# Moving two depthwise-convolution tiles from GpSimd to TensorE, tying row transposes to expert products, and adding repeated products in two norm pauses

## The chip, the cores and the metric

The kernel runs on one core of one Trainium2 chip. The metric is the device time of one execution in microseconds (us). The engines are called as in the profile: PE (TensorE), DVE (VectorE), ACT (ScalarE), POOL (GpSimd) and SP (SyncE, which here only issues transfers).

## The reference, cut to what matters

All tensors are float32. Two blocks run one after the other on 512 tokens of width 1024; the first one puts 16 meta tokens in front, so that it works on 528 rows.

The first block has two layers. Each projects the rows onto ten parts, and computes beside an indexer, a top-132 selection and an eight-head attention over the selected keys a convolution branch:

```python
def conformer_conv_branch(a, g, z, w_dw, b_dw, ln_g, ln_b):
    u = a * jax.nn.sigmoid(g)                      # 512 channels
    u = lax.conv_general_dilated(u, w_dw[:, None, :], window_strides=(1,),
        padding=[(30, 0)], feature_group_count=512, ...) + b_dw   # 31 taps
    u = jax.nn.silu(layer_norm(u, ln_g, ln_b))
    return u * jax.nn.silu(z)
...
    y = concatenate([y_conv, y_attn]) @ w_out[l]
    h = layer_norm(DEEPNORM_ALPHA * h + y, post_ln_g[l], post_ln_b[l])
```

The second block is one layer of windowed attention and a gated linear attention, then 16 experts, each of which takes the 64 tokens with the highest affinity to it (gate, up and down matrices of 1024 x 1024 each, 201 MB in all), and a gated per-token embedding.

## The kernel before

The 512 convolution channels of a layer are four tiles of 128 channels (partitions) by 528 or 512 positions. The phase `p_ag(c)` projects a and g of tile c (two projections of 48 fp32r products each) and forms `u`. From there a tile goes one of two ways. If c stands in `pconv`, `conv_tap` makes 31 taps: ACT scales a shifted view of `u` by the tap (line 333), and POOL adds the result onto `cv` (line 335); two `prod` buffers lie between them, so that ACT waits at the third tap that POOL has not taken. Otherwise `conv_operands(c)` makes 16 tiny products (line 346), one DVE product of 128 x 1024 (line 348), writes `u` to DRAM and reads it back in eight pieces with the positions shifted (lines 354 to 360, all issued by SP), and later `conv_products(c)` runs 64 fp32 products in four column groups of PE (lines 261 and 267, through `burst`) and one ACT copy (line 376). The operands of such a tile lie in buffers that exist once (`szc`, `k2l`, `side`); `szc` is also where the gate of the branch (`p_zc`) is put.

A planner in the compiler orders the instructions of each engine ahead of the run, by simulated times and by levels: of the instructions that are ready it takes the one of the highest level, and within a level the one that was written first. Each engine then runs its list strictly in order. `self.plan` gives each layer the order of its levels, the order of its phases, and `pconv`. In layer 0 the levels are `w, topk, tail, idx, proj, conv, att, ag, rest, fill`; in layer 1 `w, tail, idx, conv, proj, att, ag, topk, rest, fill`. `p_ag(c)` stands in level `ag` (after attention) if c is in `pconv`, and in `proj` (before it) if not. After the phases comes the tail: a one-element `warm` activation on `cv` of the last `ag` tile of the phase order (`clast`), a Sqrt that makes ACT load its square-root table ahead of need, the layer norm of the branch, the output projection, and the post norm.

In the experts, pair j of two experts needs its 128 token rows gathered by POOL (`gather_rows`, line 1500) and turned on PE (`gather_cols`, line 1507). These tasks are written at fixed steps of the loop over weight pieces: the turns for pair j four steps ahead of its gate products. The rows of pair 0 come from a product with a one-hot matrix instead (`first_rows`, line 1495). The expert products are line 1643; two products of 64 columns run side by side. Expert weights stream through SP into every buffer that has come free.

Of the kernel before, what the change touches and what calls it, by code (L numbers as in the profile page):

```python
# [23 lines left out]
KT = D // 128  # L24
# [45 lines left out]
class Net:  # L70
    def __init__(self, tc, I, out, dbg=None, upto=99):
        self.tc, self.nc, self.I, self.out, self.dbg = tc, tc.nc, I, out, dbg
        self.upto = upto
        self.bgq = []
        self.plan = [
            (('w', 'topk', 'tail', 'idx', 'proj', 'conv', 'att', 'ag', 'rest', 'fill'),
             ('ag0', 'idx', 'q', 'k', 'sc', 'ag3', 'v', 'cp3', 'ag2', 'ag1', 'topk', 'zc', 'att', 'za'),
             (2, 0, 1, 3),
             (2, 3, 1, 0),
             (0, 1, 2)),  # L80
            (('w', 'tail', 'idx', 'conv', 'proj', 'att', 'ag', 'topk', 'rest', 'fill'),
             ('idx', 'q', 'k', 'sc', 'ag2', 'v', 'cp2', 'ag3', 'ag1', 'cp3', 'ag0', 'topk', 'att', 'za', 'zc'),
             (2, 0, 1, 3),
             (2, 3, 1, 0),
             (0, 1)),
        ]
        self.order2 = ('w', 'crit', 'att', 'gla', 'main', 'late', 'fill')
        self.gn0, self.apull, self.gpull, self.ng = 2, 3, (1, 0, 2, 1), 0
        self.early = ("qk", "qk", "u", "szc", "cv", "qi", "xl", "xl", "parts", "v", "c1", "sm", "sm", "one", "raw", "raw", "raw", "hw", "hl")
        self.last = ("raw", "u", "szc", "qi")  # L90
        self.cycle = ("qk", "qk", "u", "szc", "cv", "qi", "xl", "xl", "v", "sm", "sm", "one", "raw", "raw", "raw", "hw", "hl")
        self.piece = 264
        self.swap = True
        self.stack = True
        self.sqsum, self.sqe, self.xlp = 'v', 'AAAAAAAA', ()
        self.pairs2 = False
        self.pairs, self.spare = False, None
        self.cur = None
        self.pos = 0
# [181 lines left out]
    def layer(self, l):  # L281
        nc, I = self.nc, self.I
# [3 lines left out]
        T = L - q0  # L286
# [218 lines left out]
        v = self.sb([128, 4, 512], "v")  # L505
# [199 lines left out]
                tmp = self.sb([128, T], "th", "rl", 3)  # L705
                self.silu2(seg(szc[0][:, e, :]), ps, seg(tmp))

        phases = dict(cp2=lambda: conv_products(2), cp3=lambda: conv_products(3), ag0=lambda: p_ag(0), ag1=lambda: p_ag(1), ag2=lambda: p_ag(2), ag3=lambda: p_ag(3), idx=p_idx, sc=p_scores, topk=p_topk, k=p_k, q=p_q, v=p_v, att=p_att, za=p_za, zc=p_zc)
        for n in seq:
            phases[n]()  # L710

# [12 lines left out]
        for t in range(nt):  # L724
            ps = self.ps([128, 512], "tp")
            for c in range(4):
                nc.tensor.transpose(ps[:tw, c * 128:(c + 1) * 128], cv[:, c, t * tw:(t + 1) * tw], self.ident)
            x = self.sb([128, 512], "xct", "pT" if t < 4 else "rl", 4 if t < 4 else 3)
# [37 lines left out]
        for e, ps in self.proj_tiles(w_out, 0, D, y, KT, fsegs if q0 == 0 else ((0, S),), half=True):  # L766
            ot = self.sb([128, T], "ot", "rl", 3)
            for k in range(2):
                nc.vector.scalar_tensor_tensor(seg(ot), seg(hT[k][:, e, q0:].bitcast(F32)), ALPHA, ps if k == 0 else seg(ot),
                                               op0=ALU.mult, op1=ALU.add)  # L770
            ec = slice(e * 128, (e + 1) * 128)
            pt = self.ps([128, 4, 128], "tp")
            for i in range(4):
                c0 = NM - q0 + 128 * i
                nc.tensor.transpose(pt[:, i, :], ot[:, c0:c0 + 128], self.ident)
            nc.scalar.copy(z[:, :, ec], pt)
            for i in range(4):
                nc.vector.bn_stats(st[:, i, e, :], z[:, i, ec])
            if l == 0:
                pm = self.ps([NM, 128], "pm")  # L780
                nc.tensor.transpose(pm, ot[:, 0:NM], self.ident)
                nc.scalar.copy(zM[:, ec], pm)
                nc.vector.bn_stats(stM[:, e, :], zM[:, ec])
        mv = self.sb([128, 5, 2], "mv")
        sc = self.sb([128, 5, 2], "sc")
        nc.vector.memset(mv, 1.0)
# [566 lines left out]
    def experts(self, mx):  # L1353
        nc, I = self.nc, self.I
# [147 lines left out]
        def gather_cols(j, st):  # L1502
            xf = self.sb([128, KT, 128], "xf", "ya", 2)
            for g in range(2):
                pt = self.ps([128, 4, 128], "tp")
                for k in range(4):
                    nc.tensor.transpose(pt[:, k, :], st["xr"][:, g * 512 + k * 128:g * 512 + (k + 1) * 128], self.ident)
                gained(xf, pt, g, gf)
            xfs[j] = xf

# [106 lines left out]
        for kind, j in streams:  # L1617
            if (kind, j) == ("d", NP - 1):
                load_gate()
            rows_of = dict(p=128) if j == 0 and kind != "d" else dict(t=KT)  # L1620
            wv = [I[names[kind]][0, 2 * j + q].rearrange("(t p) f -> p t f" if "p" in rows_of else "(p t) f -> p t f", **rows_of) for q in range(2)]
            ps = None
            for t in range(0, KT, 2):
                run_tasks(step + 1)
                if (kind, j, t) == ("d", NP - 1, KT - 2):

                    two = [self.sb([128, 2, D], "rawe", "raw", 3) for q in range(2)]
                    raw = [[[two[q][:, k, :]] for k in range(2)] for q in range(2)]
                    for k in range(2):
                        for q in range(2):  # L1630
                            nc.sync.dma_start(raw[q][k][0], wv[q][:, t + k, :])
                else:
                    raw = [chunk(w, t) for w in wv]
                if ps is None:
                    ps = self.ps([128, 2, 512], "pp", "pp", 2)
                for k in range(2):
                    x = hids[j][(t + k) // 4][:, (t + k) % 4] if kind == "d" else xfs[j][:, t + k]
                    for s in range(2):
                        for q in range(2):
                            r = raw[q][k]  # L1640
                            r = r[s] if len(r) > 1 else r[0][:, s * 512:(s + 1) * 512]
                            a = slice(64 * q, 64 * q + 64)
                            nc.tensor.matmul(ps[a, s, :], x[:, a], r, start=(t == 0 and k == 0), stop=(t == KT - 2 and k == 1), skip_group_check=True)  # L1643
                step += 2
            if kind == "g":
                at_step(step, post_gate, j, ps)
            elif kind == "u":
                at_step(step + 2, post_up, j, ps)
            else:
                at_step(step, post_down, j, ps)  # L1650
                at_step(step, scat_init, j)
                for i in range(4 if j < NP - 1 else 0):
                    for s in range(2):
                        at_step(step + 2 + 2 * (i // 2), scat, j, i, s)
# [139 lines left out]
```

## Time and profile before

| | us |
|---|---|
| median of 3 runs (1835.46 to 1839.21) | 1838.72 |
| the profiled execution, its own time | 1837.06 |
| span of that execution, first to last instruction | 1835.2 |
| PE busy | 1688.8 |
| DVE busy | 931.9 |
| ACT busy | 766.7 |
| POOL busy | 219.8 |

A busy PE is not a PE at its peak, since the ends of pipelined products are modelled. Roughly: layer 0 runs to 383 us, layer 1 to 741, the second block's mixing to 1270, the experts from 1298 to 1770, and the gated embedding to the end. The mean granted PE clock was 0.97 of 2.4 GHz.

### The profile page before, as it was taken

The page shows a single profiled execution, that of the slowest core. Times are in us where ns is not written, and L with a number is a line of the kernel's source. Part 1 is how long each engine was busy: PE and PEld are TensorE (multiplying, and loading weights), DVE is VectorE, ACT ScalarE, POOL GpSimd, SP SyncE. Part 2 cuts the span into 40 slices and gives each one's busy share as a digit, 9 for nine tenths or more (in the row PEclk, how much of TensorE's full clock was granted, in tenths as well). Part 3 has the DMA queues.
Part 4 walks back from the last instruction along what each step waited for, and adds up shares of the span by engine and source line. Part 5 has one row for each costly group of instructions (what it writes and reads, how often), then busy time and mean ns, then how long its engine had stood idle before and what let it go on. Part 6 is the DMA issues. An engine that isn't in the chain of part 4 may idle for free.

```text
span 1835.2 us, 28863 instructions
## 1 busy us (share of the span) xinstructions
PE 1688.8 (92%) x11867; PEld 1320.9 (72%) x11867; DVE 931.9 (51%) x1860; ACT 766.7 (42%) x1314; POOL 219.8 (12%) x161
## 2 busy tenths in 40 slices
PE   6999998989999999799999999998899988788888
PEld 6988896989987879798978899997533333233246
DVE  3899756566995556875534455544311221012044
ACT  3883587356526783643456453323200000000026
POOL 1620486000005740000000000000000000000000
PEclk9999998989999999899999999999999999999999
DMA  6124120121233112222113248466699999999961
GB/s 195 58 70 113 47 70 24 53 71 47 76 97 110 47 47 70 81 92 68 58 47 98 78 158 296 131 247 252 240 420 421 421 420 421 419 420 421 418 272 46
DMA packets 149461, 327.63 MB, mean 179 GB/s; under 512 B 13467, under 2 KB 103259, under 8 KB 131025
## 3 DMA queue, kind: packets, MB, share of 16 engines
q1 hardware_dynamic: 144464, 314.75, 46.7%
q10 hardware_dynamic: 3856, 7.37, 1.1%
q0 software_dynamic: 1008, 3.67, 0.5%
q8 instruction: 93, 1.52, 0.3%
q14 instruction: 40, 0.32, 0.1%
HBM read 308.58 MB, written 17.11 MB: 177 GB/s over the span
## 4 chain that ended last, share of the span: by engine, by line
PE 64%; DMA 17%; ACT 7%; DVE 6%; POOL 3%; issue 2%; ACTq 0%; DVEq 0%; POOLq 0%; SPq 0%
PE pp L182 41%; PE pp L1643 8%; DMA rawe<-in_w_exp_up 6%; DMA rawe<-in_w_exp_down 5%; DMA rawe<-in_w_exp_gate 4%; POOL cv L335 3%; PE pp L1703 2%; ACT wh L160 1%; ACT prod L333 1%; ACT smb L651 1%; PE pidx L242 1%; PE psc L1541 1%; PE po L261 1%; PE pidx L243 1%; DVE wl L161 1%
## 5 line engine op out<-in xcount | busy, mean ns | idle before, releaser
L335 POOL TENSOR_TENSOR cv<-cv,prod 128x528 f32<-128x528 f32 (+1 forms) x150 | 212.9, 1420 | 452.9 <-ACT prod L333 444.8
L1643 PE MATMUL pp<-rawe,xf 128*64 128x512 f32 x1024 | 251.0, 606 | 11.1 <-DMA rawe<-in_w_exp_gate 6.9
L160 ACT CAST wh<-raw 128x1024 fp32r<-128x1024 f32 (+2 forms) x149 | 151.0, 1016 | 253.1 <-PE pp L182 221.2
L182 PE MATMUL pp<-hTh,wh 128*128 128x264 f32 (+2 forms) x1056 | 223.3, 291 | 12.0 <-ACT th L385 9.8
L161 DVE TENSOR_TENSOR wl<-raw,wh 128x1024 fp32r<-128x1024 f32 (+2 forms) x149 | 186.6, 1253 | 92.1 <-ACT wh L160 81.9
L182 PE MATMUL pp<-hTl,wh 128*128 128x264 f32 (+2 forms) x1056 | 221.7, 289 | 0.0
L182 PE MATMUL pp<-hTh,wl 128*128 128x264 f32 (+2 forms) x1056 | 219.9, 287 | 0.0
L1643 PEld LDWEIGHTS pp<-rawe,xf 128*64 128x64 f32 x1024 | 78.4, 139 | 158.7 <-issue 133.0
L182 PEld LDWEIGHTS pp<-hTh,wh 128*128 128x128 f32 (+1 forms) x1056 | 165.4, 190 | 22.1 <-ACT th L385 12.2
L182 PEld LDWEIGHTS pp<-hTl,wh 128*128 128x128 f32 (+1 forms) x1056 | 165.7, 189 | 6.0 <-issue 5.5
L182 PEld LDWEIGHTS pp<-hTh,wl 128*128 128x128 f32 (+1 forms) x1056 | 165.5, 190 | 4.5 <-issue 4.0
L182 PE MATMUL pp<-xTh,wh 128*128 128x264 f32 (+1 forms) x752 | 153.7, 285 | 2.9 <-ACT op L1072 2.3
L182 PE MATMUL pp<-xTl,wh 128*128 128x264 f32 (+1 forms) x752 | 154.9, 285 | 0.7 <-DVE xTl L1167 0.7
L182 PE MATMUL pp<-xTh,wl 128*128 128x264 f32 (+1 forms) x752 | 154.5, 283 | 0.0
L1643 PE MATMUL pp<-rawe,hid 128*64 128x512 f32 x512 | 127.8, 617 | 19.1 <-DMA rawe<-in_w_exp_down 18.7
L1532 DVE SCALAR_TENSOR_TENSOR Y<-pp,per,Y 128x512 fp32r<-128x512 f32 x16 | 12.0, 748 | 233.5 <-ACT Y L1531 233.5
L333 ACT ACTIVATE prod<-u,taps 128x528 f32<-128x528 f32 (+1 forms) x150 | 107.3, 729 | 36.5 <-POOL cv L335 35.9
L1500 POOL DMA_INDIRECT xr<-xrows,slots x7 | 6.7, 958 | 938.8 <-DMA pled<-pe 639.4
L182 PEld LDWEIGHTS pp<-xTh,wh 128*128 128x128 f32 (+1 forms) x752 | 115.2, 189 | 4.6 <-ACT op L1072 2.5
L182 PEld LDWEIGHTS pp<-xTl,wh 128*128 128x128 f32 (+1 forms) x752 | 115.0, 188 | 3.6 <-issue 2.5
L182 PEld LDWEIGHTS pp<-xTh,wl 128*128 128x128 f32 (+1 forms) x752 | 115.1, 188 | 0.8 <-issue 0.8
L1643 PEld LDWEIGHTS pp<-rawe,hid 128*64 128x64 f32 x512 | 40.2, 141 | 100.6 <-issue 62.7
(526 smaller groups left out, 2941.7 us busy)
## 6 DMA issues: line engine op xcount, KB each, us to landing
rawe<-in_w_exp_gate SPq DMA_DIRECT2D x53, 1024.0 KB
rawe<-in_w_exp_up SPq DMA_DIRECT2D x52, 1024.0 KB
rawe<-in_w_exp_down SPq DMA_DIRECT2D x51, 1024.0 KB
raw<-in_w_in SPq DMA_DIRECT2D x45, 1024.0 KB
rawe<-in_w_exp_down SPq DMA_DIRECT2D x26, 512.0 KB
rawe<-in_w_exp_up SPq DMA_DIRECT2D x22, 512.0 KB
rawe<-in_w_exp_gate SPq DMA_DIRECT2D x22, 512.0 KB
raw<-in_w_in SPq DMA_DIRECT2D x20, 512.0 KB
```

The lines of the kernel that those rows point to most:

```text
L160: nc.scalar.copy(wh, raw_view)
L161: nc.vector.tensor_sub(wl, raw_view, wh.bitcast(F32))
L182: nc.tensor.matmul(ps[:m, s, x:min(x + k, n)], a[:, t, :m], b[:, c0 + x:min(c0 + x + k, c1)], start=(t == 0 and pi == 0 and x == 0), stop= ...
L242: nc.tensor.matmul(out, qs[:, p, x, :], kh, start=True, stop=False)
L243: nc.tensor.matmul(out, qs[:, p, x, :], kl, start=False, stop=True)
L261: first = self.nc.tensor.matmul(*args, **kw)
L333: nc.scalar.activation(pr, src, AF.Identity, scale=taps[:, c, j + 1:j + 2], bias=0.0 if j else cvec[:, c, 31:32])
L335: nc.gpsimd.tensor_tensor(cv[:, c, :], cv[:, c, :], pr, op=ALU.add)
L651: nc.scalar.activation(sm[:, x, :], sm[:, x, :], AF.Exp, bias=mx[:, h:h + 1], scale=0.125, accum_out=ssum[:, h:h + 1])
L1541: nc.tensor.matmul(ps, ohts[j][:, 128 * i:128 * (i + 1)], Ys[j][:, k, s * 512:(s + 1) * 512], start=(k == 0), stop=(k == 1))
L1643: nc.tensor.matmul(ps[a, s, :], x[:, a], r, start=(t == 0 and k == 0), stop=(t == KT - 2 and k == 1), skip_group_check=True)
L1703: nc.tensor.matmul(ps[k][:, k, :], a[:, t, :], wp[t][:, w, k * 512:(k + 1) * 512], start=(t == 0 and pi == 0), stop=(t == KT - 1 and pi == 2))
```

## The change

Three edits. First, the plan: in layer 0 tile 2 leaves `pconv` and gets the phases `ag2`, `cp2` behind `ag1`; in layer 1 tile 1 leaves it and gets `ag1`, `cp1` behind `ag0`. Five of eight tiles are then products instead of three. `clast` changes with the phase order: in layer 0 from tile 1 to tile 2, in layer 1 from tile 0 to tile 1, both of them tiles that are now products. Second, each turn in `gather_cols` is placed behind the expert product written last (`issue_after` orders two instructions of one engine in its list). Third, after the output projection of a layer, 12 or 8 products of the last `ot` tile with itself go into a PSUM tile that nobody reads.

```diff
-             ('ag0', 'idx', 'q', 'k', 'sc', 'ag3', 'v', 'cp3', 'ag2', 'ag1', 'topk', 'zc', 'att', 'za'),
+             ('ag0', 'idx', 'q', 'k', 'sc', 'ag3', 'v', 'cp3', 'ag1', 'ag2', 'cp2', 'topk', 'zc', 'att', 'za'),
...
-             (0, 1, 2)),
+             (0, 1,)),
...
-             ('idx', 'q', 'k', 'sc', 'ag2', 'v', 'cp2', 'ag3', 'ag1', 'cp3', 'ag0', 'topk', 'att', 'za', 'zc'),
+             ('idx', 'q', 'k', 'sc', 'ag2', 'v', 'cp2', 'ag3', 'ag0', 'cp3', 'ag1', 'cp1', 'topk', 'att', 'za', 'zc'),
...
-             (0, 1)),
+             (0,)),
...
+        hot = self.ps([128, 128], "hot")
+        for k in range(12 if l == 0 else 8):
+            nc.tensor.matmul(hot, ot[:, 0:128], ot[:, T - 128:T], start=True, stop=True)
...
-                    nc.tensor.transpose(pt[:, k, :], st["xr"][:, g * 512 + k * 128:g * 512 + (k + 1) * 128], self.ident)
+                    with self.tc.issue_after(self.latest.ins):
+                        nc.tensor.transpose(pt[:, k, :], st["xr"][:, g * 512 + k * 128:g * 512 + (k + 1) * 128], self.ident)
...
-                            nc.tensor.matmul(ps[a, s, :], x[:, a], r, start=(t == 0 and k == 0), stop=(t == KT - 2 and k == 1), skip_group_check=True)
+                            self.latest = nc.tensor.matmul(ps[a, s, :], x[:, a], r, start=(t == 0 and k == 0), stop=(t == KT - 2 and k == 1), skip_group_check=True)
```

## Rows read from the trace of the kernel before

**Rows 1.** The page, moved data per 1/40 of the span.

```profile
GB/s 195 58 70 113 47 70 24 53 71 47 76 97 110 47 47 70 81 92 68 58 47 98 78 158 296 131 247 252 240 420 421 421 420 421 419 420 421 418 272 46
```

**Rows 2.** Windows by stage: length, PE, PEld, DVE, ACT, POOL, clock, DMA, GB/s.

```profile
182.00:312.00 130.00, 123.05 (x1021) 105.57 (x1012) 83.63 (x229) 93.12 (x190) 84.11 (x60) 0.96 0.15 50
430.00:547.00 117.00, 114.14 (x994) 108.16 (x992) 107.99 (x243) 60.83 (x102) 0.00 (x0) 0.99 0.27 73
547.00:676.00 129.00, 122.08 (x1144) 105.61 (x1143) 70.61 (x185) 93.44 (x189) 80.95 (x60) 0.99 0.25 76
```

**Rows 3.** The chain of waits between 560 and 700 us, shares by line.

```profile
by line: POOL cv L335 33.7%; PE pp L182 21.0%; ACT prod L333 6.6%; ACT smb L651 6.2%; issue 5.0%; ACT wh L160 4.9%; ACT pT L618 2.5%; DVE wl L161 2.4%; PE tp L727 1.5%; PE po L267 1.4%; ACT th L755 1.2%; DVE smb L646 1.1%; PE tp L616 1.1%; 
```

**Rows 4.** ACT's waits, 182 to 312, then 547 to 676: total us, times, longest.

```profile
ACT prod L333 <- POOL cv L335: 14.1, 17, 2.3
...
ACT prod L333 <- POOL cv L335: 17.5, 27, 1.5
```

**Rows 5.** Timeline of PE, products of one tile: start, us, instruction, count.

```profile
141.13 0.35 PE L346 MATMUL pcv<-taps,base 128*32 128x8 f32 x18
...
174.18 0.42 PE L267 MATMUL pp<-us,cwt 128*32 128x264 f32 x3
...
177.55 0.40 PE L267 MATMUL pp<-us,cwt 128*32 128x264 f32 x3
...
178.53 0.42 PE L267 MATMUL pp<-us,cwt 128*32 128x264 f32 x3
...
181.89 0.40 PE L267 MATMUL pp<-us,cwt 128*32 128x264 f32 x3
```

**Rows 6.** The waits of SP's queue between 60 and 345 us.

```profile
SPq L152 <- DVE wl L161: 170.9, 12, 52.5
```

**Rows 7.** Timeline of ACT, its table loads in the two tails.

```profile
310.41 1.28 ACT L723 ACT_TABLE_LOAD   x1
...
318.97 1.28 ACT L734 ACT_TABLE_LOAD   x1
...
684.03 1.28 ACT L277 ACT_TABLE_LOAD   x1
```

**Rows 8.** Timeline at the first expert pair, in brackets the idle time before.

```profile
1298.42 7.41 PE L1495 MATMUL tp<-oh,z 128*128 128x128 f32 x64 [1.40 <-DVE oh L1490]
...
1305.60 1.08 POOL L1500 DMA_INDIRECT xr<-xrows,slots  x1 [639.40 <-DMA pled<-pe]
1305.87 0.69 DVE L1480 TENSOR_TENSOR xf<-tp,gains 128x512 f32<-128x512 f32 x1 [2.16 <-PE tp L1495]
...
1309.95 0.30 PE L1507 MATMUL tp<-base,xr 128*128 128x128 f32 x1 [4.12 <-DMA xr<-xrows,slots]
...
1310.18 3.62 PE L1643 MATMUL pp<-rawe,xf 128*64 128x512 f32 x8
```

**Rows 9.** Windows at the same place.

```profile
1308.00:1312.00 4.00, 2.05 (x7) 0.73 (x9) 0.00 (x0) 0.00 (x0) 0.00 (x0) 0.77 0.30 112
1312.00:1316.00 4.00, 4.00 (x18) 1.26 (x16) 0.00 (x0) 0.00 (x0) 0.00 (x0) 0.80 0.00 0
1316.00:1320.00 4.00, 4.00 (x20) 1.26 (x18) 0.00 (x0) 0.00 (x0) 0.00 (x0) 1.00 0.88 305
```

**Rows 10.** Timeline of PE at the two post norms.

```profile
387.08 1.00 PE L810 MATMUL pm<-base,zM 16*128 16x16 f32 x8 [4.54 <-ACT z L801]
388.01 3.67 PE L818 MATMUL tp<-base,z 128*128 128x128 f32 x16
...
392.21 0.60 PE L818 MATMUL tp<-base,z 128*128 128x128 f32 x4
...
742.84 3.65 PE L1160 MATMUL tp<-base,z 128*128 128x128 f32 x16 [4.00 <-DVE z L799]
```

**Rows 11.** Windows at the first post norm.

```profile
390.00:392.00 2.00, 2.00 (x11) 2.00 (x11) 1.13 (x2) 1.98 (x3) 0.00 (x0) 0.50 0.00 0
392.00:394.00 2.00, 2.00 (x19) 2.00 (x19) 2.00 (x4) 2.00 (x5) 0.00 (x0) 1.00 0.00 0
```

More of the change, by code (lines that the diff above doesn't have):

```diff
@@ L706, in p_zc @@
                 self.silu2(seg(szc[0][:, e, :]), ps, seg(tmp))
-        phases = dict(cp2=lambda: conv_products(2), cp3=lambda: conv_products(3), ag0=lambda: p_ag(0), ag1=lambda: p_ag(1), ag2=lambda: p_ag(2), ag3=lambda: p_ag(3), idx=p_idx, sc=p_scores, topk=p_topk, k=p_k, q=p_q, v=p_v, att=p_att, za=p_za, zc=p_zc)
+        phases = dict(cp0=lambda: conv_products(0), cp1=lambda: conv_products(1), cp2=lambda: conv_products(2), cp3=lambda: conv_products(3), ag0=lambda: p_ag(0), ag1=lambda: p_ag(1), ag2=lambda: p_ag(2), ag3=lambda: p_ag(3), idx=p_idx, sc=p_scores, topk=p_topk, k=p_k, q=p_q, v=p_v, att=p_att, za=p_za, zc=p_zc)
         for n in seq:
```

## The prediction, made before the changed kernel was built or run

> **What bounds the kernel now.** I read the page's line of moved data first. From the slice at about 1330 us to 1743 us it stands at 418 to 421 GB/s [rows 1]: the expert weights stream at a constant rate, so the end of that stretch is fixed by when the stream starts and by the bytes left, and PE's own pauses in it cost nothing. Ahead of it the rate is far lower, and whatever shortens the two layers moves the start of the stream, and with it the end, one for one.
>
> Second, the windows by stage. Both layers have a stretch of attention with conv taps under it, 182 to 312 and 547 to 676 us [rows 2]. PE is busy 123.05 of 130 us and 122.08 of 129 us, ACT about 93 us, POOL 84 and 81 us. The reader is to see two things: PE has little idle time there (6.95 and 6.92 us), but it is less densely loaded than its busy time says, since its weight loads fill 105.6 us of each stretch, 0.81 and 0.82, against 108.16 of 117 us (0.924) where only projections run.
>
> Third, the chain of waits in layer 1's stretch: a third of it is POOL at line 335 [rows 3], and ACT stands 14.1 and 17.5 us in its own queue behind a tap that POOL has not taken [rows 4]. Exponentials queue behind those taps. Fourth, the start of the experts [rows 8, 9], and fifth, the two post norms [rows 10, 11].
>
> **The turns of gathered rows.** PE ends pair 0's row products at 1305.83 us (1298.42 + 7.41). The next PE instruction is one single turn of pair 1's rows, and it waits 4.12 us for a gather that POOL issued only at 1305.60 [rows 8]. Behind it stand all expert products; nothing else holds them: pair 0's second half of rows is finished at 1306.56 (1305.87 + 0.69) and is wanted four steps in. The first product starts at 1310.18 instead of about 1305.85: 4.33 us lost. After the pause the clock is at 1.2 GHz for part of the next 8 us; granted means of 0.77 and 0.80 [rows 9] are a shortfall of (0.23 + 0.20) x 4 = 1.72 us of full-speed work, and the first products take 3.62 us for eight. All loaded buffers are full by then: no byte moves from 1312 to 1316, and 305 GB/s in the next 4 us mean, at 420, a restart at 1317.1 [rows 9]. The restart waits for the first buffer that products release, so it moves by both terms: 4.33 + 1.72 = 6.05 us, taken as 6.1. The edit puts the turn behind the products of the step before, where the gather has long landed; most of the pair's other turns stand there already by the planner's own choice. Bounds: 4.3 if the clock falls anyway, 6.1 in full, and 0 if the weights or rows of the first product are what is really late, which the 0.23 us between turn and product speaks against. I take 6.1, since the stream behind it is saturated to the end.
>
> **Two conv tiles on PE.** Removed in each layer: 30 POOL adds and 31 ACT activations. Of the 60 taps of the stretch, half go, so ACT and POOL are relieved of about a third and a half of what they do there [rows 2, 4]. Added to PE: 64 fp32 products in two runs, 174.18 to 177.77 and 178.53 to 182.1, 7.2 us, and 32 tiny instructions, 18 of which take 0.35 us, so 0.6 us [rows 5]; 7.8 us for each layer, 15.6 in all. One more DVE product and one ACT copy are hidden under stretches where neither engine is full. Nine more transfers go into SP's queue, and the read-back waits for the write; behind them stand weight loads, which now wait 170.9 us for free buffers anyway [rows 6]. If that cover went, a projection would start late by one such round trip. Moved: the projection of the tile, and its products, from behind attention to ahead of it. Its PE work is the same, but it is no longer there to fill attention's pauses.
>
> What PE gets back is unknown, so I bound it. Nothing recovered: +15.6 us. At the other end, both stretches become as dense in weight loads as the projection stretch: 105.6 / 0.924 = 114.2, plus 7.8, is 122.0 us against 130 and 129, so -8.0 and -7.0, together -15.0 us. Between them: the idle time and the half-clock time of the stretches are 6.95 + 0.04 x 130 = 12.1 us and 6.92 + 0.01 x 129 = 8.2 us, 20.3 together [rows 2]. If all is recovered the edit is worth -4.7, if half, +5.4. ACT's relief is larger than these pauses, but attention loses filler, so I take the middle, +0.4 us.
>
> Perfetto Trace Analysis of the Trainium skill (Identifying the Most-Contended Engine) says that matmul busy time is a bad measure of headroom and weight-load time a better one. By busy time the products find 14 us of room, by weight loads 47; the sum would be +0.4 by the first reading and -15.0 by the second, which is the first rival below.
>
> **The Sqrt warm-up.** `warm` reads `cv` of tile `clast` and stands in level `tail`, above attention. Before, layer 0's `clast` ends on POOL with attention, and its table load at 310.41 falls right ahead of the norm. After, that tile is a product, done early, so the load comes in the midst of the exponentials, forces their table back, and the norm must load Sqrt itself, just ahead of its Silu load at 318.97. One load is 1.28 us [rows 7]: +1.3 us on layer 0's tail. In layer 1 the norm loads Sqrt itself already, at 684.03, so nothing is added on that tail. The loads amid attention are ACT time that the removed taps pay for (below nothing is excluded; above, three more loads are 3.8 us).
>
> ScalarE: Activation LUTs of the Trainium skill (Table sets: the hidden batching unit) says to do all functions of one table set before switching, and prices a switch at about 2.7 us; the row's 1.28 us is less than half of that, and by the page the term would be 2.7 and the sum 1.4 us later.
>
> **Repeated products.** Each fp32 product is two passes (128 instructions for 64 products above). A 128-column pass is 0.22 us at 1.2 GHz (3.67 us for 16) and about 0.11 at 2.4 (0.60 us for 4, the last drained) [rows 10]. Twelve products are 24 passes, 5.3 us at the low level, in a pause of 4.54 us: up to 0.8 us late. If they bring the clock back, the work from 387.08 to 392, which now runs at 0.50 [rows 11], gains up to half of its 5.1 us, 2.6 us; layer 1 has 16 passes in a pause of 4.00 us, and its 16 turns at 3.65 us could gain 1.8 us [rows 10]. But ACT, which evicts these turns, is full in those windows (1.98 and 2.00 of 2 us), so they may only wait elsewhere. So -1.0 and -0.5 us, -1.5 in all, between +0.8 and -4.4.
>
> **Sum.** 1837.06 - 6.1 + 0.4 + 1.3 - 1.5 = 1831.2 us, against the profiled execution's own time; the median of the runs, 1838.72, lies 1.7 above that execution. I predict 1831.
>
> **Rivals.** *Denser than it looks (faster).* Freed of 30 taps, ACT and POOL no longer pace attention, and PE packs products into short stalls that its busy time hides. For it: rows 3 and 4, and 0.81 against 0.924. Against: attention mixes small fp32 products and turns that load PE differently. Time: 1837.06 - 6.3 - 15.0 = 1815.8.
>
> *Attention only starts later (slower).* The projection of the extra tile and its products go ahead of attention, which starts later, keeps its length, and has less filler under it, so that all 15.6 us are paid: 1837.06 - 6.3 + 15.6 = 1846.4. For it: PE's idle share is 5% only. Against: half of the taps are gone from attention's own chain. It decides from where less than 4.0 us of the 15.6 come back (slower than 1842.4 is 11.2 above the sum, that is conv at 0.4 + 11.2 = 11.6).
>
> *The turn does not help.* The planner puts something else ahead of the first product, or the stream restarts when it did: 1831.2 + 6.1 = 1837.3, no change.
>
> **How the numbers follow.** About 0.2%, 3.7 us, is what a measurement of this kernel can tell from no change, so faster is below 1835.0 and slower above 1842.4. The forecast (1825 to 1835) has 0.47, the dense rival (below 1825) 0.23, no change (the third rival, or conv costs of 4 to 11 us) 0.17, the slower rival 0.13. Faster 0.70, same 0.17, slower 0.13. The range for 8 in 10 reaches to both outer rivals, 1816 to 1845; the forecast's own is 1825 to 1835.
>
> **What would show it.** In the changed profile the first expert product should follow pair 0's rows without a wait, near a clock of 1.00, and the 420 GB/s begin some 5 us after it. POOL's line 335 should show 90 adds; the two stretches should show ACT near 70 us and the wait for POOL halved; a Sqrt load and one back should stand amid layer 0's attention, and another ahead of the norm. The low-clock window behind each post norm should be shorter. I am wrong if attention's end moves later against the start of its layer by more than 5 us, if the turn only changes places with another wait, or if the products in the pause run into the turns behind them.

## The result and the profile after

The changed kernel takes 1849.02 us (median, 1846.73 to 1852.9), the kernel before 1837.51 beside it: ratio 1.0061, 95% interval 1.0046 to 1.0076, some 11 us slower. I had forecast 1831. The profiled execution is the longest one, 1852.9 us, so its rows stand about 4 us above the median.

Where the time went is read from landmarks of the two traces: TensorE's first projection product, the end of attention in each layer (its last DVE product, L680), the last turn of each output projection, the first expert product, the end. Lengths in us:

| stretch | before | after | difference |
|---|---|---|---|
| layer 0, start to attention's end | 290.7 | 295.1 | +4.3 |
| layer 0, attention's end to last turn | 70.2 | 69.8 | -0.4 |
| layer 1, last turn to attention's end | 295.3 | 309.9 | +14.6 |
| layer 1, attention's end to last turn | 61.1 | 60.4 | -0.7 |
| last turn to first expert product | 571.5 | 569.0 | -2.5 |
| first expert product to the end | 525.0 | 524.7 | -0.3 |

The differences sum to 15.0 us in these two executions, more than the 11 us between the medians. So the loss lies in the two stretches of attention, some three quarters of it in layer 1. The turn's gain is seen only in part in the last two lines; what hides it is told at the end of this document.

The page of the changed kernel, moved data per 1/40 of the span: the saturated stretch has its old rate [rows 1] and its old length; it is only later.

```profile
GB/s 194 58 69 113 77 47 47 44 72 54 75 96 109 54 47 69 100 69 92 42 57 75 76 144 295 164 213 232 260 421 420 421 421 420 421 420 420 418 270 46
```

The windows by stage (columns as in [rows 2]; the stages end later, so they are longer):

```profile
182.00:317.00 135.00, 129.53 (x1201) 112.81 (x1194) 80.65 (x235) 77.30 (x163) 43.07 (x30) 0.99 0.20 59
430.00:552.00 122.00, 119.14 (x1019) 112.20 (x1018) 108.94 (x241) 64.15 (x106) 0.00 (x0) 0.97 0.25 67
552.00:697.00 145.00, 134.17 (x1297) 113.50 (x1296) 66.98 (x193) 77.84 (x161) 39.53 (x30) 0.96 0.26 77
```

ACT and POOL are relieved (ACT 93 to 77 us, where I had put some 70; POOL from over 80 to 43 and 40). Layer 0's stretch is denser, 0.84 of it in weight loads against 0.81. Layer 1's is emptier, 113.50 of 145 = 0.78, with 10.8 us of PE idle time against 6.92. Its waits (total us, times, longest), first those of PE, then ACT's for DVE and POOL:

```profile
PE pidx L261 <- ACT pT L618: 6.2, 1, 6.2
PE pp L261 <- DMA side<-ud: 2.0, 1, 2.0
PE po L261 <- ACT pT L618: 1.5, 1, 1.5
...
ACT smb L651 <- DVE mx L648: 24.1, 10, 6.0
...
ACT prod L333 <- POOL cv L335: 12.0, 19, 1.5
```

and before, PE's longest one and ACT's for DVE:

```profile
PE pp L182 <- ACT th L385: 3.5, 1, 3.5
...
ACT smb L651 <- DVE mx L648: 2.9, 4, 1.1
```

ACT's wait for POOL fell only from 17.5 to 12.0 us [rows 4], though half the taps went; its new waits are for DVE, 24.1 us where they were 2.9, that is for scores that PE has not made. The largest pause, in ACT's timeline:

```profile
594.51 0.72 ACT L333 ACTIVATE prod<-u,taps 128x512 f32<-128x512 f32 x1
595.68 0.72 ACT L333 ACTIVATE prod<-u,taps 128x512 f32<-128x512 f32 x1 [0.45 <-POOL cv L335]
597.88 0.72 ACT L333 ACTIVATE prod<-u,taps 128x512 f32<-128x512 f32 x1 [1.48 <-POOL cv L335]
599.22 0.72 ACT L333 ACTIVATE prod<-u,taps 128x512 f32<-128x512 f32 x1 [0.62 <-POOL cv L335]
599.85 1.03 ACT L160 CAST wh<-raw 128x1024 fp32r<-128x1024 f32 x1
600.78 0.60 ACT L385 ACTIVATE th<-pp 128x528 f32<-128x528 f32 x1
601.28 0.47 ACT L618 COPY pT<-tp 128x384 f32<-128x384 f32 x1
```

PE's next scores need the PSUM buffer that this copy at 601.28 empties (scores and turned probabilities share four); the copy stands behind four taps that go at POOL's pace, a weight cast and the late tile's tanh. Only then does the late tile's trip begin, in SP's queue, and PE's products wait for it (timeline of both):

```profile
601.80 1.00 PE L261 MATMUL pidx<-qk 64*128 64x384 f32 x1 [6.23 <-ACT pT L618]
...
603.60 0.34 SPq L354 DMA_DIRECT2D ud<-u  x1
...
609.63 0.43 SPq L360 DMA_DIRECT2D side<-ud  x1
...
614.20 0.63 PE L261 MATMUL pp<-side,cwt 128*32 128x256 f32 x1 [1.97 <-DMA side<-ud]
```

The windows from the pause to the end of the products show the clock after the pause (0.57) and under the products (0.81), which is why they take 8.88 us here. The pause alone does not settle that: in e11 (below) the same 64 products stand behind a pause of 6.3 us and run at 1.00, in 7.32 us. In the changed kernel:

```profile
600.00:608.00 8.00, 6.20 (x36) 4.43 (x38) 5.36 (x14) 7.22 (x17) 6.03 (x6) 0.57 0.34 114
...
614.00:623.00 9.00, 8.80 (x128) 8.12 (x128) 0.00 (x0) 1.45 (x2) 4.36 (x4) 0.81 0.01 2
```

The start of the experts, timeline of PE, against [rows 8]: the first expert product follows the rows of its pair with no wait.

```profile
1317.53 8.94 PE L1498 MATMUL tp<-oh,z 128*128 128x128 f32 x64 [1.40 <-DVE oh L1493]
1326.40 4.08 PE L1647 MATMUL pp<-rawe,xf 128*64 128x512 f32 x18
```

The windows there, against [rows 9]: full clock, and the bytes are back at their full rate some 6 us after the first product (363 GB/s in the second window), against 7 before.

```profile
1328.00:1332.00 4.00, 4.00 (x20) 1.29 (x18) 0.00 (x0) 0.00 (x0) 0.00 (x0) 1.00 0.30 76
1332.00:1336.00 4.00, 4.00 (x22) 1.40 (x20) 0.00 (x0) 0.00 (x0) 0.00 (x0) 1.00 0.94 363
```

ACT's table loads in layer 0 stand where I had put them, a Sqrt load and one back amid attention, and two ahead of the norm (Sqrt and Silu) where [rows 7] have one:

```profile
236.91 1.28 ACT L723 ACT_TABLE_LOAD   x1
...
247.81 1.28 ACT L271 ACT_TABLE_LOAD   x1
...
323.29 1.28 ACT L277 ACT_TABLE_LOAD   x1
324.81 1.28 ACT L734 ACT_TABLE_LOAD   x1
```

Layer 0's post norm, timeline of PE, against [rows 10]:

```profile
387.11 3.71 PE L786 MATMUL hot<-ot 128*128 128x128 f32 x24
391.86 0.64 PE L813 MATMUL pm<-base,zM 16*128 16x16 f32 x8 [1.03 <-ACT z L804]
392.43 2.03 PE L821 MATMUL tp<-base,z 128*128 128x128 f32 x16
395.40 0.66 PE L821 MATMUL tp<-base,z 128*128 128x128 f32 x4 [0.95 <-DVE tt L826]
```

and one window there, against [rows 11]:

```profile
391.00:395.00 4.00, 2.60 (x24) 2.28 (x24) 3.50 (x9) 4.00 (x6) 0.00 (x0) 1.00 0.00 0
```

The clock is back at 1.00 and 16 turns take 2.03 us, not 3.67; but ACT, which empties them, is busy 4.00 of 4 us, and PE now waits. The last of the norm's 32 turns ends 15.0 us behind the last turn of the output projection (14.7 before), and layer 1's first projection product starts 9.0 us behind it, as before.

### The profile page after: what moved, and what is told of

Its sections match the earlier page's. It is cut to its first block, busy times and chain, and to the rows that moved or that the text cites. A ratio compares the mean times of both kernels' runs of the same rounds, so it can differ in the third digit from the quotient of the medians.

```text
span 1851.1 us, 29461 instructions
## 1 busy us (share of the span) xinstructions
PE 1712.6 (93%) x12227; PEld 1338.9 (72%) x12227; DVE 921.0 (50%) x1862; ACT 732.3 (40%) x1256; POOL 137.3 (7%) x101
## 3 DMA queue, kind: packets, MB, share of 16 engines
q0 software_dynamic: 1008, 3.67, 0.5%
## 4 chain that ended last, share of the span: by engine, by line
PE 68%; DMA 18%; DVE 5%; ACT 5%; issue 2%; POOL 1%; SPq 0%; ACTq 0%; DVEq 0%; POOLq 0%
PE pp L182 42%; PE pp L1647 8%; DMA rawe<-in_w_exp_down 6%; DMA rawe<-in_w_exp_gate 5%; DMA rawe<-in_w_exp_up 4%; PE pp L1707 2%; PE pp L267 2%; POOL cv L335 1%; PE tp L616 1%; PE po L261 1%; PE pidx L261 1%; PE pidx L242 1%; PE psc L1545 1%; PE pidx L243 1%; DMA side<-ud 1%
## 5 line engine op out<-in xcount | busy, mean ns | idle before, releaser
L335 POOL TENSOR_TENSOR cv<-cv,prod 128x528 f32<-128x528 f32 (+1 forms) x90 | 130.4, 1449 | 487.7 <-ACT prod L333 481.3
L1529 ACT COPY hid<-tp 128x512 f32<-128x512 f32 x16 | 8.7, 588 | 184.5 <-PE tp L1527 184.3
```

Of the source, the lines that this page charges most:

```text
L335: nc.gpsimd.tensor_tensor(cv[:, c, :], cv[:, c, :], pr, op=ALU.add)
```

## The experiments

Each was timed in five rounds beside the kernel before. Times below are the ratio less one, times 1838 us, so "-6.2" means 6.2 us under before; an interval is some 2 to 3 us to each side. TensorE's order is planned anew when a kernel is built, so every edit may also shift work that it does not name. e5, e8, e9, e10, e14 and e16 leave out part of the convolution, or its right operands, to price what is left. "Late tile" is the tile that the change moved: tile 2 in layer 0, tile 1 in layer 1.

**The parts.** The turn alone, then turn and repeated products (the plan put back), then the tile in one layer only.

```diff
 # e1_turn_only: the kernel before with
+                    with self.tc.issue_after(self.latest.ins):
...
 # e2_turn_and_hot: the changed kernel with self.plan of before
 # e3_tiles_layer0, e4_tiles_layer1: the changed kernel with one layer's plan of before
```

> The kernel before with the turn edit alone. Theory (the step of the prediction): the first expert product stands right behind the rows of its pair and the saturated stream restarts earlier, so 6 us faster than before, ratio 0.9967. Rival (the turn changes places with another wait, and the gain seen in the changed kernel came from the tiles): no change, ratio 1.000.

> The changed kernel with the plan of the tiles put back: turn edit and repeated products alone. Against the run with the turn edit alone this gives the price of the repeated products. My step: 1.5 us faster than with the turn edit alone (7.5 us faster than before, ratio 0.9959). Rival (the turns after the pause wait for ACT's evictions, so the clock gives nothing and the products in the pause run into them): level with the turn edit alone or up to 1 us slower. If the tiles are what made the changed kernel slow, this kernel is about 19 us faster than the changed one, ratio 0.9955 to 0.997 against before.

> The changed kernel with layer 1's plan put back, so the extra conv tile as products in layer 0 alone. Theory A (each layer pays by where its late products fall in TensorE's order: layer 0's stretch still had a hole of 12 us to fill, layer 1's had not): 5 us over the run with turn and repeated products. Rival B (only the added work counts, the same in both layers): 9 us over it.

> The changed kernel with layer 0's plan put back, so the extra conv tile as products in layer 1 alone. Theory A: 14 us over the run with turn and repeated products. Rival B (only the added work counts, the same in both layers): 9 us over it.

e1: 1832.86 us, 0.9966 (0.9953 to 0.9979), -6.2: the turn is worth what I had worked out, and this is the fastest kernel that leaves nothing out; it beats both. In its trace the last two stretches of the first table are 567.0 and 523.2 us, 4.5 and 1.8 under before, against the 4.33 and 1.72 of my sum. e2: 0.9983 (0.9974 to 0.9993), -3.1. Between e1 and e2 the traces have the same 295.3 and 295.5 us from layer 0's last turn to layer 1's attention end: at layer 0's norm the repeated products gain nothing. From layer 1's last turn to the first expert product they have 567.0 and 567.2; as e2's products of pair 0's rows happen to take 8.90 us there, not 7.41, a gain of 1.2 us at layer 1's norm may be hidden. What e2 loses lies elsewhere, between layer 1's attention end and its last turn, 64.2 us against 61.1, where the same code got another order: the turns at L754 come later, and PE then waits 2.28 us, not 0.67, for ACT's `ych`. e3: 1.0008 (0.9994 to 1.0022), 4.6 over e2. e4: 1.0050 (1.0032 to 1.0069), 12.3 over e2. The layers do not pay alike, as theory A had it.

**Is it the trip?** The late tile's products on other data, their place behind or ahead of other work, and their number.

```diff
 # e5_no_trip, in conv_operands
+            if c == {0: 2, 1: 1}[l]:
+                ready[c] = w, [u[:, c, q0:q0 + nx]] * 4
+                return
 # e6_products_behind_za: layer 1's plan; products in level 'rest'
-... 'cp3', 'ag1', 'cp1', 'topk', 'att', 'za', 'zc'
+... 'cp3', 'ag1', 'topk', 'att', 'za', 'cp1', 'zc'
 # e7_ag1_first: layer 1's plan
-... 'ag3', 'ag0', 'cp3', 'ag1', 'cp1', 'topk'
+... 'ag3', 'cp3', 'ag1', 'ag0', 'cp1', 'topk'
 # e8_few_products: late tile with
+                for e in range(1):
```

> The changed kernel, but the products of the second tile that each layer does on PE late (tile 2 of layer 0, tile 1 of layer 1) read the tile's own rows, not the copy that goes out to DRAM and comes back in four shifted groups: the same number and shape of products, no write, no eight read-backs, no wait for the single operand buffer. This leaves out the right operands of that convolution. Theory A (the operands of the late tile come after a round trip of some 10 us during which PE's written order holds nothing that may run, so PE starves and falls to the low clock): 10 us faster than the changed kernel, 6 of it in layer 1. Rival B (only the added product work counts, attention starts later by it and nothing is recovered): level with the changed kernel, at most 3 us faster.

> The changed kernel with layer 1's late products written behind the four gate projections of attention, in the same low level, so that four projections may run while the operands travel. Same work, same transfers. Theory A: most of layer 1's starved time comes back, 8 us faster than the changed kernel. Rival B: level, or slower, because the tile's own result reaches the norm later.

> The changed kernel with layer 1's late tile projected ahead of the POOL tile's projection, so that the two projections of the POOL tile (about 11 us of PE) stand between the late tile's operands and its products. Theory A: the trip is covered, 6 us faster than the changed kernel. Against it works that POOL's 30 adds start some 10 us later; if POOL's chain decides, no gain. Rival B: level with the changed kernel.

> The changed kernel with 8 of the 64 products for the late tile of each layer: one eighth of the convolution's taps is computed, the operands, the trip and the buffers stay. Product work falls by 6.3 us in each layer. Rival B (each us of product work is paid): 12.6 us faster than the changed kernel. Theory A: the wait ahead of the products stays, so layer 1 gives back the 6.3 us behind it and layer 0, which still has idle time, less: 8 to 12 us.

e5: 1.0044 (1.0032 to 1.0057), 3.1 under the changed kernel, and the intervals overlap: theory A asked for 10. The waits for the DMA (2.0 and 2.7 us) are gone from its trace, the pause of 6.2 us is not. e6: 1.0074 (1.0048 to 1.0100), not faster; its six executions spread from 1844.22 to 1860.3 us. e7: 1.0106 (1.0091 to 1.0121), 8.3 slower; attention does end 8 us earlier after layer 0's last turn (302.0 against 309.9), but the projections that had filled it then stand behind it (72.3 us to the last turn against 60.4). Theory A falls as the main cause. e8: 1.0004 (0.9992 to 1.0015), 10.5 faster for 112 products less. That lies within theory A's 8 to 12 and near rival B's 12.6, so it does not part them; I took it for rival B, that product work is simply paid, and was misled, as the next two groups show.

**Is it POOL, or the order of taps?**

```diff
 # e9_relief_only: on e1; late tile only
+            for j in range(1 if c == {0: 2, 1: 1}[l] else W31):
 # e10_no_pool_taps: on the changed kernel; all POOL tiles
+            for j in range(1):
 # e11_taps_below_attention: layer 1's levels
-('w', 'tail', 'idx', 'conv', 'proj', 'att', 'ag', ...
+('w', 'tail', 'idx', 'proj', 'att', 'conv', 'ag', ...
 # e12_warm_reads_pool_tile
+        clast = pconv[-1]
```

> The kernel with the turn edit alone, in which tile 2 of layer 0 and tile 1 of layer 1 stay on ACT and POOL but only their first tap is computed: 30 of 31 taps of each are left out, no products come in their place. This is the relief of the tiles by itself, against the turn edit alone (0.9966 of before). Theory C (PE's work bounds both stretches, so relief of ACT and POOL is worth little and every us of product work is paid): 0 to 4 us faster than the turn edit alone. Rival D (the step of the prediction: relief gives back half of the 20 us of pauses and slow clock, and something else in the changed kernel eats it): 8 to 12 us faster.

> The changed kernel, in which the tiles that stay on ACT and POOL (two in layer 0, one in layer 1) compute only their first tap: 30 of 31 taps of each are left out. Theory C: the pauses of TensorE that are left behind ACT's queue go (6.2 and 2 us in layer 1, some 4 in layer 0), the product work stays: 6 to 12 us faster than the changed kernel, still not much under before. Rival D (pauses come from the trip of the operands, not from POOL): 0 to 3 us faster.

> The changed kernel with layer 1's level for the taps put below that of attention, so that ACT's queue has evictions and exponentials ahead of taps; the one POOL tile has 75 us to spare there. Same work. Theory C: the pause of 6.2 us at 595.6 us and most of what stands behind it goes, 6 us faster than the changed kernel. Against: with its pauses gone elsewhere PE is still the bound, and the order only moves them, 0 to 2 us.

> The changed kernel with the early Sqrt reading the last POOL tile again instead of the product tile in layer 0. My step: the table load ahead of layer 0's norm goes away, 1.3 us faster than the changed kernel (2.7 us by the Trainium skill, ScalarE: Activation LUTs, Table sets: the hidden batching unit), and the profile shows no table load at that norm's Sqrt. Rival (the load hides beside other engines' waits): level.

e9: 0.9930 (0.9917 to 0.9943), 6.6 faster than e1: relief is worth more than theory C's 4 us at most, and less than rival D's 8 at least. e10: 1.0023 (1.0005 to 1.0041), 7.0 under the changed kernel, which is within theory C's 6 to 12 and still slower than before with no conv add left on POOL. e11: 1.0059, level; the planner gave ACT the same order, and the pause is still there at 6.3 us, so it tells nothing of what another order would bring. e12: 1.0074 (1.0054 to 1.0094), level; it is no test of the table load, since the POOL tile that it reads is done at 256 us too, and both loads ahead of the norm stayed.

**Two by two, then the move.** By then the parts did not add up: the changed kernel is 14.3 us over e2, and products at about 12 (e8, for all 128), trip 3 and relief -6.6 leave some 6 us without a place. So the products were put beside the taps with no operands (they read rows that are there early), with and without relief, and then the late tile's projection was moved alone.

```diff
 # e13_products_without_relief: on e1; in the plans ('ag2', 'ag1', 'dp2', ...), ('cp3', 'ag0', 'dp1', ...)
+        def added_products(c):
...
+                        products.append(((ps[32 * g:32 * g + 32, k, :n], self.ident[:, 32 * g:32 * g + 32], u[:, c, x0:x0 + n]), ...
 # e14_products_and_relief: e13 with the line of e9
 # e15_tiles_without_hot: the changed kernel
-            nc.tensor.matmul(hot, ot[:, 0:128], ot[:, T - 128:T], start=True, stop=True)
 # e16_move_only: e14 with ('ag1', 'ag2', 'dp2', ...), ('ag0', 'cp3', 'ag1', 'dp1', ...) and
+            self.go("ag" if c in pconv and c != {0: 2, 1: 1}[l] else "proj")
 # e17_tiles_inside_attention: e15, late tile's projection and products
-            self.go("proj")
+            self.go("ag")
```

> The kernel with the turn edit alone, plus 64 products of the conv tile's shape in each layer, at the written place of the changed kernel's late products; they read rows that are there early and their result is not used, so no operands are made and nothing travels. All taps stay on ACT and POOL. Against the turn edit alone (0.9966 of before): if PE bounds both stretches, the products are paid at their measured 7.3 to 8.9 us in each layer, 14 to 17 us slower. If the pauses take them in, 0 to 6 us slower.

> The same added products, with 30 of 31 taps of tile 2 of layer 0 and tile 1 of layer 1 left out: products and relief together, no operands, no trip. If the two add, this stands at the products alone less 6.6 us. If relief is worth nothing once PE has more work, it stands level with the products alone (at most 2 us faster).

> The changed kernel without the repeated products: turn edit and tiles. Against products and relief together this adds operands, trip and their waits: 4 to 6 us slower. Against the changed kernel: level if the repeated products are worth nothing in themselves and the 2.6 us between the runs with the turn edit alone and with both came of another order of layer 1's tail; 2 to 3 us faster if they cost time wherever they stand.

> The kernel of e14 (added products on rows that are there early, 30 of 31 taps of the late tile left out, no operands, no trip) with the late tile's projection moved as in the changed kernel: written behind the other POOL tile's, and in the level ahead of attention. If the move is the price of the tiles, this stands 9 to 12 us above e14 (about 1843, ratio 1.002 to 1.004). If the operands are, it is level with e14 (0.997).

> The changed kernel without the repeated products, with the late tile's projection and its products put into the level below attention, where the projection stood before. Operands, trip and products are all there. If the move is the price, most of it comes back: 8 to 12 us faster than e15 (1.0054), ratio about 0.999 to 1.001. If the operands and their single buffers are, it is level with e15 or slower, since the products come later and the gate projections of the conv behind them too.

| kernel | what it has | ratio (95%) | us to before |
|---|---|---|---|
| e1 | turn | 0.9966 (0.9953 to 0.9979) | -6.2 |
| e9 | turn, relief | 0.9930 (0.9917 to 0.9943) | -12.9 |
| e13 | turn, products | 1.0018 (1.0008 to 1.0028) | +3.3 |
| e14 | turn, relief, products | 0.9969 (0.9953 to 0.9985) | -5.7 |
| e16 | e14 and the move | 1.0010 (0.9997 to 1.0022) | +1.8 |
| e15 | e16 with real operands and trip | 1.0054 (1.0037 to 1.0070) | +9.9 |
| after | e15 and repeated products | 1.0061 (1.0046 to 1.0076) | +11.2 |
| e17 | e15 with the move taken back | 1.0147 (1.0123 to 1.0171) | +27.0 |

Products cost 9.6 us without relief; relief gives 6.6 without products and 9.0 with them; together they cost 0.5 us. They do add, and the missing us were elsewhere: 7.5 in the move (e16 less e14), 8.1 in operands, trip and the copy of the result (e15 less e16). e17 came out by the second half of its expectation, level or slower, but at 17 us over e15, a size that I had not foreseen: with the tile back below attention, operands, products and the gate projections behind them all come late. So it shows that the move can't simply be taken back, and does not price the move by itself; that the two prices can't be avoided one by one with this order of work is argued from it, not shown.

From the first projection product to layer 0's last turn, and from there to layer 1's, the profiled executions have:

| us | e1 | e9 | e13 | e14 | e16 | e15 | after |
|---|---|---|---|---|---|---|---|
| layer 0 | 359.4 | 353.5 | 363.7 | 357.6 | 364.3 | 363.7 | 364.9 |
| layer 1 | 356.4 | 356.9 | 362.6 | 359.4 | 362.8 | 368.2 | 370.3 |

By these the move is 10.1 us, 6.7 of it in layer 0, and operands and trip are 4.8, all in layer 1: one execution each, so the two prices are known to some 3 us. Relief by itself (e9 less e1) is all in layer 0. In layer 1 of e9 attention ends 7.3 us earlier behind layer 0's last turn (288.0 against 295.3), but projections are left for behind it (68.9 us to the last turn against 61.1): there a shorter attention only moved work behind itself. ACT's table loads are not the move's price: layer 0 has four in e9, e14, e16 and e15 alike, and layer 1 one fewer in e16 than in e14.

What the move does is seen in PE's timeline, first score to the start of the last product with v; for layer 1 counted from layer 0's last turn. Attention begins at 169.5 us in before, 169.3 in e14, 171.8 in e16, 169.5 in e15, 171.1 after: it starts at most 2.5 us later. It lasts 124.4, 118.9, 128.6, 136.9 and 137.4 us: it is stretched by what has been put into its midst. (e14 leaves some projections for behind attention: 69.9 us to the last turn, not 61.1.) In layer 0 it lasts 112.9 us in e14 and 120.5 in e16, with 69 us behind it in both, so there the move is paid in full. PE's windows of attention's stretch, both layers, of e1:

```profile
182.00:309.00 127.00, 120.10 (x985) 103.35 (x984) 80.63 (x220) 91.74 (x188) 84.15 (x60) 0.96 0.16 51
544.00:675.00 131.00, 124.03 (x1163) 107.60 (x1161) 72.36 (x189) 94.29 (x190) 81.10 (x60) 0.99 0.24 74
```

and of e14:

```profile
182.00:309.00 127.00, 126.17 (x1168) 108.36 (x1161) 81.11 (x231) 77.42 (x163) 41.41 (x30) 1.00 0.16 51
551.00:680.00 129.00, 124.20 (x1203) 104.30 (x1201) 62.53 (x178) 82.73 (x169) 39.91 (x30) 0.99 0.20 61
```

In layer 0 of e14 the idle 6.9 us of 127 became 0.8, the clock went from 0.96 to 1.00, and the products (7.3 us from 218.76) are inside the same length: the pauses were to be had. The waits of PE in layer 1's stretch tell the rest; e14 has only short ones,

```profile
PE tp L629 <- ACT smb L664: 1.6, 2, 1.0
PE pp L261 <- ACT th L398: 1.5, 2, 1.2
PE pidx L261 <- DVE mx L659: 1.1, 1, 1.1
```

and e15 has those of the changed kernel, a pause of 6.8 us and 1.9 us for the trip:

```profile
PE pidx L261 <- ACT pT L618: 6.8, 1, 6.8
PE po L261 <- ACT pT L618: 2.1, 2, 1.5
PE pp L261 <- DMA side<-ud: 1.9, 1, 1.9
```

Why the order with operands puts ACT's copy of pT behind the late tile's casts and tanh, and the order of e16 does not, was not tried; that products which outrank attention pull casts and tanh forward is only argued. The edit that covers both prices was not found.

## Why the prediction was wrong, point by point

**The turn of gathered rows** was right in mechanism and size: -6.1 worked out, -6.2 measured (e1), and both of its terms are in e1's trace (4.5 and 1.8 us). The rival that the wait only changes places is out.

**Two conv tiles** is the step that failed. Its balance came out, "+0.4" for products against what PE gets back, +0.5 measured (e14 less e1, intervals of some 3 us), but by luck: I had 15.6 us paid and 15.2 recovered, a middle between bounds 30 us apart, and the runs have 9.6 paid and 9.0 recovered. What failed are the edits beside it that I costed at nothing. One is "Its PE work is the same, but it is no longer there to fill attention's pauses": the second half of that sentence got no price of its own, and it is 7.5 us. The other is that operand making ("are hidden") and nine transfers (behind them weight loads that wait anyway) got no price either; I named the price of one round trip for the case that the cover went, and did not see that the late tile's operands are made one after the other, from single buffers, at the very place where PE's fixed order has nothing else. This is 8.1 us (4.8 in the profiles), of which the trip is about 3 (e5); the rest goes, as far as the traces show, with the pause on ACT (6.8 us in e15, none such in e16), and why that order arises stays open. Together the term is +16.1 (e15 less e1), where my bound "nothing recovered: +15.6" stood, though relief did give its 9 us: that bound held PE's work only and no new wait. The products' own length was not the error: 7.3 us for a tile in e15 against the 7.2 read, and 8.8 at a lower clock in the changed kernel.

I had asked for the ACT and POOL figures as evidence. POOL's 90 adds came out; ACT is at 77 us, not near 70, and its wait for POOL fell from 14.1 to 7.8 us in layer 0, but only from 17.5 to 12.0 in layer 1. They show that the relief is real and nothing of what it is worth. The line that I had set against myself, attention's end against its layer's start later by over 5 us, is where the loss shows: +4.3 and +14.6.

Perfetto Trace Analysis of the Trainium skill (Identifying the Most-Contended Engine) has weight loads as the measure of the room; the estimate that I worked out by it was -15.0 for this term (the room so counted is 24.4 + 23.4 = 47.8 us, not 47). In e14 its direction is right for layer 0 (weight loads 103.35 to 108.36 us in the same 127); in the changed kernel the room was not to be had, since new waits and not density set the time.

**The rivals.** "Attention only starts later" came within 3 us of the time, 1846.4, which is luck, by a mechanism that is only half there: its projection and products do go ahead and cost filler, but attention starts where it did, to 2.5 us, and is stretched instead, product work is paid at 9.6 and not 15.6 us, and relief gives nearly all of that back. "Denser than it looks" has a true half, 6.6 to 9.0 us of relief.

**The Sqrt warm-up.** The loads moved as said, 1.28 us each; PE's wait for the first rows of the output projection grew from 1.8 to 2.8 us. But attention's end to last turn is 69.8 us against 70.2, and e9 and e14, which have the same two loads ahead of that norm, have 69.2 against 70.1 in e1. So no run shows the +1.3 of the sum, and none separates it. ScalarE: Activation LUTs of the Trainium skill (Table sets: the hidden batching unit) would have put 2.7 us there; the trace has 1.28 in every row, and the next activation starts right behind (247.81 to 249.10 us).

**Repeated products.** The step as put, "they may only wait elsewhere", is what happened; the -1.5 that I still took is not seen: in layer 0 the clock comes back and ACT takes the time, in layer 1 at most 1.2 us may be hidden (e2 against e1), and changed less e15 is +1.3, inside the intervals. My bound of +0.8 held the products' own length only (24 passes took 3.71 us, not 5.3, as the clock rose under them); e2 is 3.1 over e1 by an order that changed 60 us away from one of them.

## What to carry to other kernels

Work that is moved from a filler's place to ahead of the chain that it filled has a price of its own, even if its length is the same: price the pause that it leaves and the chain that it stands in, and try the move alone. Before a balance of work added against work removed is believed, follow the latest tile through its single buffers, queues and copies to the first product, and ask what the bound engine's fixed order holds meanwhile. An edit that plans an order anew can cost 3 us in a place that it does not touch, so price parts by landmarks in the trace and not by totals alone.

## What the runs showed that was not expected

From layer 1's last turn to the first expert product the code is the same in all kernels (but for the turn and the 8 repeated products), yet with the turn edit that stretch took from 565.7 to 573.9 us. Part of the difference sits in TensorE's granted clock. One window of 40 us, 200 us behind that turn, and the next one, in e1

```profile
935.70:975.70 40.00, 37.78 (x253) 33.33 (x253) 15.85 (x29) 20.10 (x31) 0.00 (x0) 0.91 0.34 99
975.70:1015.70 40.00, 37.67 (x265) 34.21 (x265) 18.52 (x35) 19.62 (x27) 0.00 (x0) 0.96 0.25 74
```

and in the changed kernel:

```profile
957.40:997.40 40.00, 38.80 (x224) 33.73 (x225) 13.96 (x25) 18.13 (x27) 0.00 (x0) 0.79 0.32 93
997.40:1037.40 40.00, 37.67 (x276) 33.84 (x275) 17.11 (x32) 20.54 (x28) 0.00 (x0) 1.00 0.22 73
```

0.12 x 40 = 4.8 us of full-speed work, of which the next window gives 0.04 x 40 = 1.6 back. The profiles of e6, e7, e8, e10, e11, e12, e14, e17 and the changed kernel have 0.79 there, the ten others 0.89 or 0.91; the nine need 560.2 us or more from that turn to the products that make pair 0's rows, the ten 559.7 or less. What decides between them was not found.

Those products differ too: 7.41 us at full clock in before and e1, 8.94 in the changed kernel, whose windows there are

```profile
1316.00:1320.00 4.00, 2.60 (x13) 2.48 (x12) 2.75 (x9) 3.14 (x3) 0.00 (x0) 0.67 0.95 298
1320.00:1324.00 4.00, 4.00 (x35) 4.00 (x34) 0.34 (x1) 0.06 (x1) 0.00 (x0) 0.90 0.91 345
```

That is 1.5 of the 2.0 us by which the changed kernel's fifth line lies over e1's; the clock in the 560 us ahead of it comes to the same in both, since the changed kernel has 0.91, not 0.83, in the first 40. Why the last stretch is 524.7 us and not e1's 523.2 was not traced.

DVE's subtraction that makes a weight's low part takes 1.22 us with POOL idle and from 1.3 up to 2.27 us beside POOL's adds (timeline of DVE, before):

```profile
558.59 1.22 DVE L161 TENSOR_TENSOR wl<-raw,wh 128x1024 fp32r<-128x1024 f32 x1
...
655.96 2.27 DVE L161 TENSOR_TENSOR wl<-raw,wh 128x1024 fp32r<-128x1024 f32 x1 [4.87 <-ACT wh L160]
```

In the pause at 595 us both meet: DVE's two took 2.09 and 2.05 us, and ACT waited 1.48 us for one POOL add where 0.65 is usual.
